# Layer 0 of a two-layer mixture-of-experts block: the outputs of 18 of 43 jobs are added to their tokens' rows in memory by indirect DMAs

## The chip, the cores and the metric

The kernel runs on one core of one Trainium2 chip. The metric is the device time of one execution in microseconds (us), as the median of several runs. The core has TensorE (PE, with its weight loads PEld), VectorE (DVE), ScalarE (ACT), GpSimd (POOL) and SyncE (SP); DMAs are issued here from SP's queue (plain loads) and from POOL's queue (all indirect DMAs and a few plain ones), and run on 16 DMA engines that both queues share.

## The reference, cut to what matters

Two layers follow each other over 256 latent tokens and 256 context tokens of width 1024. Each has a mixer and then a mixture of experts; layer 0 runs its experts over all 512 tokens, and it is the only layer that the change touches. A router picks 8 of 64 experts for each token; every expert is a small gated network, and a token's result is the weighted sum of its 8 experts' outputs, plus that of one shared expert:

```python
def moe_ffn(h, w_router, e_bias, w_gate, w_up, w_down, s_gate, s_up, s_down):
    scores = jax.nn.sigmoid((h @ w_router).astype(jnp.float32))
    _, idx = lax.top_k(scores + e_bias.astype(jnp.float32), TOP_K)
    wts = jnp.take_along_axis(scores, idx, axis=-1)
    wts = wts / wts.sum(-1, keepdims=True) * ROUTE_SCALE
    ...
    def expert_block(args):
        tok, e = args
        xb = h_pad[tok]
        a = jax.nn.silu(xb @ w_gate[e]) * (xb @ w_up[e])
        return a @ w_down[e]
    ...
    routed = jnp.zeros((n_tok + 1, d), h.dtype).at[slot_tok].add(y)[:n_tok]
    shared = (jax.nn.silu(h @ s_gate) * (h @ s_up)) @ s_down
    return routed + shared
```

The line with `.at[slot_tok].add(y)` is what the change does in another way for a part of the outputs.

## The kernel before, in words

**Jobs.** Layer 0 sorts its experts by load and packs them into 43 jobs of 128 slots (class `Plan`). A slot is one token of one expert. A *single* job holds one expert on four lanes of 32 slots; a *pair* job holds two segments, for two experts, of 64 and 64 or of 96 and 32 slots. Single jobs are 0, 1, 2, 6, 11, 15, 20, 25, 29, 34 and 39; all others are pair jobs.

**One iteration of the job loop** (L1685 on) for job j does, in TensorE's order: the gate and up products (`gate_up`, L1291, or `gate_up3` for single jobs, three products of split float32 parts in L161 to L163); four transposes (L1406) of job j+1's gathered rows; a part of the scatter of earlier jobs (L1464); two transposes (L1254) of the activation `a` (ScalarE's `s`, L1238, then VectorE's product, L1239); four more transposes of job j+1 and another part of the scatter; then the down products (L1302, or `down3`). The rows of job j+2 are gathered by an indirect DMA of POOL (`gather`, L1392) from `h2d` in memory, by the token numbers `idx`, into one of two buffers `xg`.

**Combining.** `place` splits a job's output into two float32r parts `yy` (ScalarE casts the high part, VectorE subtracts for the low part, L157) and builds a one-hot matrix `ss` of the slots' tokens (L1441). Every two placed jobs form a group (`GRP` = 2). `scatter` then yields 8 pieces, one for each of 4 token tiles and 2 column halves; a piece is 4 products of 128x128 by 128x512 (two jobs, two parts) and one addition into `acc` by VectorE (L1456). The loop takes 4 pieces in each iteration (`n_piece`), two behind the gate and up products and two behind the transposes of `a`, so that 16 products fall to each job.

**Single jobs** need their weights split: `gu_parts` does it for two rows of blocks at a time (`jj` = 0, 2, 4, 6), with `wh` cast by ScalarE and `wl` subtracted by VectorE (`jj` = 0) or by POOL (`jj` = 2 and 6); `jj` = 4 writes both halves into one tile `parts`. `down3` lets POOL make the `wl` of the second half.

**What sets the order.** TensorE's and SP's instructions stand in the order of the program. The other engines' instructions are ordered by the scheduler. All queues run in order: an instruction that waits holds what stands behind it. SP issues all weight loads and waits for the buffers: 11 `w8` buffers of 1 MB hold weights. Two more pools matter: `t8`, four buffers of 8 KB per partition, for `yy` and `parts`; and `k4`, 13 buffers of 4 KB per partition, for activations, `wh`, `wl`, `acc` and loads of rows.

## Time and profile before

| | |
|---|---|
| median of 3 runs | 1728.12 us (1727.6 to 1729.35) |
| the profiled execution | 1727.71 us, span 1725.8 us |
| busy: PE / PEld | 1620.1 us (94%) / 982.1 us (57%) |
| busy: DVE / ACT / POOL | 802.7 us (47%) / 481.3 us (28%) / 232.7 us (13%) |
| L1464, combining products of both layers | 912 recorded, 243.4 us |
| HBM read / written | 528.44 MB / 6.37 MB |

The page gives each engine's busy time, the span in 40 slices, the DMA queues and the costliest groups of instructions by line. Matmuls are pipelined, so a row's duration overlaps the next row's: what a product costs is read from the distance of the starts. Layer 0's job loop lies roughly between 340 and 970 us of the span, layer 1's from about 1200 us to the end.

### The profile page before, as it was taken

What the parts mean: (1) busy time and instruction counts of PE and PEld (TensorE: products, weight loads), DVE (VectorE), ACT (ScalarE), POOL (GpSimd) and SP (SyncE); (2) the same over time, 40 slices, a digit from 0 to 9 for tenths busy, and PEclk for the clock granted to TensorE, in tenths of its full rate; (3) what the DMA queues carried; (4) which work ended last, traced back from release to release, by engine and by line L of the source; (5) the groups of instructions that cost most, each with busy time, mean ns of one, the idle gap of its engine ahead of it and who ended that gap; (6) DMA issues with size and microseconds to landing.
All of it is one profiled execution on the core that took longest, in us unless ns stands there. A gap on an engine that the chain in (4) does not pass through costs nothing. (4 is left out here: it accounts for less than half of the span.)

```text
span 1725.8 us, 27915 instructions
## 1 busy us (share of the span) xinstructions
PE 1620.1 (94%) x10494; PEld 982.1 (57%) x10494; DVE 802.7 (47%) x2043; ACT 481.3 (28%) x932; POOL 232.7 (13%) x171
## 2 busy tenths in 40 slices
PE   6999999899999999999999799999999999989885
PEld 3765677555455454554545377766656655546553
DVE  2576584655466463443433761446533332222216
ACT  2446211323233232231332242422222111112111
POOL 1014141312022020220211100031100000000001
PEclk9999999999999999999999999999999999999998
DMA  9845755769888999889998567227779999999993
GB/s 330 317 173 184 267 207 207 267 235 349 319 337 304 368 344 345 325 310 361 355 350 335 195 246 260 107 91 315 281 297 421 419 420 420 420 420 420 420 420 141
DMA packets 135400, 530.90 MB, mean 308 GB/s; under 512 B 13488, under 2 KB 22208, under 8 KB 103648
## 3 DMA queue, kind: packets, MB, share of 16 engines
q1 hardware_dynamic: 125776, 500.72, 75.6%
q0 software_dynamic: 9488, 28.37, 4.6%
q8 instruction: 84, 1.38, 0.3%
q14 instruction: 52, 0.43, 0.1%
HBM read 528.44 MB, written 6.37 MB: 310 GB/s over the span
## 5 line engine op out<-in xcount | busy, mean ns | idle before, releaser
L1284 PE MATMUL bank<-w,xT 128*32 128x256 f32 (+2 forms) x2560 | 219.9, 397 | 28.5 <-DMA w<-in_moe_w_up_dram 24.8
L1464 PE MATMUL bank<-yy,ss 128*128 128x512 f32 x912 | 243.4, 404 | 1.9 <-DVE yy L157 1.6
L1302 PE MATMUL bank<-w,aT 128*32 128x512 f32 (+2 forms) x1232 | 233.6, 596 | 1.7 <-ACT aT L1258 1.7
L1291 PE MATMUL bank<-w,xT 128*32 128x512 f32 (+2 forms) x1456 | 233.5, 594 | 0.0
L1239 DVE SCALAR_TENSOR_TENSOR a<-s,wsl,bank 128x256 f32<-128x256 f32 x71 | 34.1, 480 | 398.6 <-ACT s L1238 398.6
L1284 PEld LDWEIGHTS bank<-w,xT 128*32 128x32 f32 (+2 forms) x2560 | 130.3, 125 | 116.2 <-DMA w<-in_moe_w_up_dram 32.4
L1456 DVE TENSOR_TENSOR acc<-acc,bank 128x512 f32<-128x512 f32 x220 | 149.0, 684 | 78.4 <-PE bank L1464 77.5
L1464 PEld LDWEIGHTS bank<-yy,ss 128*128 128x128 f32 x912 | 161.8, 189 | 35.3 <-DVE yy L157 3.4
L1238 ACT ACTIVATE s<-bank 128x256 f32<-128x256 f32 x71 | 27.3, 384 | 508.0 <-PE bank L1291 226.2
L157 DVE TENSOR_TENSOR yy<-bank,yy 128x512 fp32r<-128x512 f32 x140 | 96.2, 688 | 129.3 <-ACT yy L157 129.3
L1291 PEld LDWEIGHTS bank<-w,xT 128*32 128x32 f32 (+2 forms) x1456 | 70.9, 122 | 145.2 <-issue 136.6
L157 ACT CAST yy<-bank 128x512 fp32r<-128x512 f32 x140 | 81.9, 586 | 244.5 <-PE bank L1302 205.3
L1302 PEld LDWEIGHTS bank<-w,aT 128*32 128x32 f32 (+2 forms) x1232 | 67.6, 123 | 118.7 <-issue 110.1
L1392 POOL DMA_INDIRECT xg<-h2d,idx x43 | 49.8, 1158 | 491.6 <-PE bank L1406 388.0
L1214 DVE TENSOR_SCALAR oh<-ib,pos 128x64 bf16<-128x64 bf16 (+3 forms) x428 | 84.2, 272 | 12.9 <-PE bank L1225 12.8
L157 DVE TENSOR_TENSOR wl<-half,wh 128x1024 fp32r<-128x1024 f32 x35 | 49.9, 1429 | 69.2 <-ACT wh L157 69.2
L1384 POOL TENSOR_TENSOR xr<-xr,tmp 128x512 f32<-128x512 f32 x4 | 6.3, 1580 | 537.5 <-DVE tmp L1383 537.5
L157 POOL TENSOR_TENSOR wl<-w,wh 128x1024 fp32r<-128x1024 f32 x28 | 67.9, 2425 | 38.1 <-ACT yy L157 13.9
L161 PE MATMUL bank<-wh,hT 128*128 128x512 f32 x160 | 66.3, 414 | 2.7 <-ACT wh L157 2.1
L163 PE MATMUL bank<-wl,hT 128*128 128x512 f32 x160 | 64.2, 401 | 3.0 <-DVE wl L157 3.0
L162 PE MATMUL bank<-wh,hT 128*128 128x512 f32 x160 | 64.0, 400 | 0.3 <-DVE hT L157 0.2
L1432 PE MATMUL bank<-ohr,h2p 128*128 128x256 f32 x448 | 61.0, 289 | 0.6 <-DVE ohr L1421 0.5
(362 smaller groups left out, 2382.5 us busy)
## 6 DMA issues: line engine op xcount, KB each, us to landing
w<-in_moe_w_down_dram SPq DMA_DIRECT2D x104, 1024.0 KB, 12.9
w<-in_moe_w_gate_dram SPq DMA_DIRECT2D x128, 512.0 KB, 7.0
w<-in_moe_w_up_dram SPq DMA_DIRECT2D x128, 512.0 KB, 7.7
w<-in_moe_w_gate_dram SPq DMA_DIRECT2D x64, 1024.0 KB, 17.4
w<-in_moe_w_up_dram SPq DMA_DIRECT2D x64, 1024.0 KB, 17.3
w<-in_w_mod_dram SPq DMA_DIRECT2D x24, 1024.0 KB, 12.0
half<-in_na_w_in_dram SPq DMA_DIRECT2D x12, 1024.0 KB, 9.4
mh<-in_w_mod_dram SPq DMA_DIRECT2D x12, 1024.0 KB, 5.2
```

The lines of the kernel that those rows point to most:

```text
L157: return A.copy(o_h, src), eng.tensor_sub(o_l, src, o_h.bitcast(F32))
L161: T.matmul(p, xh, wh, start=first, stop=False)
L162: T.matmul(p, xl, wh, start=False, stop=False)
L163: T.matmul(p, xh, wl, start=False, stop=last)
L1214: V.tensor_scalar(oh[:, 32 * lane:32 * (lane + m)], ib[:, off:off + 32 * m], pos[:, t, c:c + 1], None, op0=OP.is_equal)
L1284: T.matmul(p[sl, q * FF:q * FF + FF], xT(j, sl), ws[k][0][q][:, j], start=j == 0, stop=j == NJ - 1, **kw)
L1291: T.matmul(p[sl], xT(j, sl), ws[k][0][j // 4][:, :, j % 4, :], start=j == 0, stop=j == NJ - 1, **kw)
L1302: T.matmul(p[sl], aT[:, j, sl], d[:, n * 512:n * 512 + 512], start=j == 0, stop=j == 1, **kw)
L1392: G.indirect_dma_start(out=x, out_offset=None, in_=h2d[:n2, :], in_offset=bass.IndirectOffsetOnAxis(ap=idx_col, axis=0), bounds_check=n2 - ...
L1432: T.matmul(o, h2p[t][k][:, 2 * q + j], oh[:, t].rearrange("p a b -> p (a b)")[:, :n], start=t == 0 and k == 0, stop=t == nt - 1 and k == 1)
L1456: add = {0: lambda t, r, p: V.tensor_add(acc[t][:, r], acc[t][:, r], p)}
L1464: T.matmul(p, ss[:, t * 128:t * 128 + 128], yy[:, q, r], start=k == 0 and q == 0, stop=k == len(grp) - 1 and q == 1)
```

## The change

Eighteen jobs, the odd ones from 3 to 37 of layer 0 (`sent`), are no longer placed and scattered. `send` copies such a job's output to a tile `yd` (of `t8`) and POOL adds its rows to rows of a tensor `accd` in memory by an indirect DMA with an add, one for each segment: 14 of the 18 are pair jobs with two such DMAs, four are single jobs with one. The second segment's token numbers have to lie on partitions from 0 on, so `second` forms them by small products (`idx2`). Empty slots go to 128 spare rows of `accd`, by `token_index`. `accd` is set to zero by five stores of 512 KB at the start of layer 0. `fetch` reads a tile of 128 tokens back and adds it to `acc`, in each of jobs 38 to 41. With a group of two placed jobs now coming every four jobs, `n_piece` is halved from job 2 to job 39.

```diff
--- before.py
+++ after.py
@@ -1019,6 +1019,7 @@
 
     h2d = dp.tile([512, D], F32, name="h2d")
     xd = dp.tile([512, D], F32, name="xd")
+    accd = dp.tile([640, D], F32, name="accd")
 
     def moe(l, out_of, nt, mp, pre=lambda: None, post=lambda: None):
         n2 = nt * 128
@@ -1186,10 +1187,20 @@
         tok = mp.tile([128, njob], F32, name="tok")
         idx = mp.tile([128, njob], I32, name="idx")
 
+        sent = range(3, njob - 4, 2) if l == 0 else ()
+        idx2 = mp.tile([96, njob], I32, name="idx2")
+
+        def token_index(i_, t_, e_):
+            V.tensor_scalar(e_, t_, 0.0, pid[:t_.shape[0]], op0=OP.is_equal, op1=OP.mult)
+            V.scalar_tensor_tensor(i_, t_, FAR, e_, op0=OP.add, op1=OP.add)
+
         def slot_info(sl, w_, t_, i_):
             V.reduce_sum(w_, sl[:, :, 0:3], axis=AX.X)
             V.tensor_add(t_, sl[:, :, 3], sl[:, :, 4])
-            V.tensor_scalar(i_, t_, FAR, None, op0=OP.add)
+            if l:
+                V.tensor_scalar(i_, t_, FAR, None, op0=OP.add)
+            else:
+                token_index(i_, t_, sl[:, :, 0])
 
         n0 = max(j for j in range(njob) if jobs[j][0][0] < NS) + 1
         group = [0, n0, n0 + 4] + list(range(n0 + 4 + SG, njob, SG)) + [njob]
@@ -1215,12 +1226,25 @@
                                         None, op0=OP.is_equal)
                     ohs[j].append(oh)
 
+            def second(j):
+
+                c, lane, m, off = jobs[j][1]
+                o = p[:32 * m, 256 + 2 * (j - j0):258 + 2 * (j - j0)]
+                for t, oh in enumerate(ohs[j]):
+                    T.matmul(o, oh[:, 32 * lane:32 * (lane + m)], wt[:, t, c, 3:5], start=t == 0, stop=t == nt - 1)
+                tk = mp.tile([96, 2], F32, name="tk2", tag="tk2", bufs=2)[:32 * m]
+                V.tensor_copy(tk, o)
+                V.tensor_add(tk[:, 0:1], tk[:, 0:1], tk[:, 1:2])
+                token_index(idx2[:32 * m, j:j + 1], tk[:, 0:1], tk[:, 1:2])
+
             marks(j0)
             for j in range(j0, j1):
                 if j + 1 < j1:
                     marks(j + 1)
                 yield
                 c0 = min(sg_[0] for sg_ in jobs[j])
+                if j in sent and len(jobs[j]) > 1:
+                    second(j)
                 for t, oh in enumerate(ohs.pop(j)):
                     T.matmul(p[:, (j - j0) * 15:(j - j0) * 15 + 15], oh, wt[:, t, c0:c0 + 3, :],
                              start=t == 0, stop=t == nt - 1)
@@ -1352,6 +1376,8 @@
             xgs = [k4([128, D], f"xg{i}") for i in range(2)]
             for x in xgs:
                 V.memset(x, 0.0)
+            for t in range(nt + 1):
+                G.dma_start(accd[t * 128:t * 128 + 128, :], xgs[t % 2])
 
         def both(xs, j0, xT):
             for k in range(2):
@@ -1452,6 +1478,22 @@
                     V.tensor_mul(y, ps[n], times[:, r])
                 split(yy[:, 0, r], yy[:, 1, r], y)
             return yy, ss if ss is not None else tokens(t_col)
+
+        def send(j, ps):
+
+            y = t8([128, D], "yd", F32)
+            A.copy(y[:, :512], ps[0])
+            V.tensor_copy(y[:, 512:], ps[1])
+            for k, (c, lane, m, off) in enumerate(jobs[j]):
+                i_ = (idx2 if k else idx)[:32 * m, j:j + 1]
+                G.indirect_dma_start(out=accd[:, :], out_offset=bass.IndirectOffsetOnAxis(ap=i_, axis=0),
+                                     in_=y[32 * lane:32 * (lane + m)], in_offset=None, compute_op=OP.add)
+
+        def fetch(t):
+
+            y = k4([128, D], "ad")
+            S.dma_start(y, accd[t * 128:t * 128 + 128, :])
+            V.tensor_add(acc[t], acc[t], y)
 
         add = {0: lambda t, r, p: V.tensor_add(acc[t][:, r], acc[t][:, r], p)}
 
@@ -1583,7 +1625,6 @@
         for sg_ in jobs:
             passes.append(3 if l == 0 and len(sg_) == 1 and sg_ is not jobs[0] else 4)
         grp, sc = [], iter(())
-        n_piece = -(-2 * nt // GRP)
         over = overflow()
         LA = 3 if l == 0 else 2
         with tc.manual_schedule(engines={mybir.EngineType.SP, mybir.EngineType.PE}):
@@ -1684,6 +1725,9 @@
                     early[c] = expert_dn(c, ds(S.value_load(ordi[0:1, c:c + 1], min_val=0, max_val=NE - 1), 1))
             for j in range(njob - l):
                 segs = jobs[j]
+                n_piece = -(-2 * nt // GRP)
+                if sent and 2 <= j < njob - 3:
+                    n_piece //= 2
                 experts([sg_[0] for sg_ in segs])
                 if j == njob - 1:
                     g2s = [modrow(l, "g2", s) for s in range(nt // 2)]
@@ -1751,7 +1795,12 @@
                     for _ in sc:
                         pass
                     add_x = add[0] = fold(g2s)
-                grp.append(place(ps, tok[:, j:j + 1]))
+                if j in sent:
+                    send(j, ps)
+                else:
+                    grp.append(place(ps, tok[:, j:j + 1]))
+                if sent and 0 <= j - (njob - 5) < nt:
+                    fetch(j - (njob - 5))
                 if len(grp) == GRP or j >= njob - 2:
                     for _ in sc:
                         pass
```

The scheduler and the pools place the new instructions. In the rows below, a wait on DMASW is for the landing of a DMA that POOL issued, one on DMAHW for one that SP issued, and the digit tells the semaphore; `_49` is a suffix of all.

POOL's queue around job 20, a single job, before (`xg` the gathers, `wl` the low parts of job 20's weights):

```order
L1392 DMA xg_1813<-h2d,idx 128x1024 [waits DMASW5_49,PE_49]
L1392 DMA xg_1812<-h2d,idx 128x1024 [waits DMASW6_49,PE_49]
L157 TENSOR_TENSOR wl<-w_5744,wh 128x1024 [waits DMAHW3_49,DMAHW2_49,Activation_49]
L157 TENSOR_TENSOR wl<-w_5747,wh 128x1024 [waits DVE_49,DMAHW4_49,PE_49,DMAHW5_49,Activation_49,Pool_49]
L1392 DMA xg_1813<-h2d,idx 128x1024 [waits DMASW7_49,PE_49]
L157 TENSOR_TENSOR wl<-w_5750,wh 128x1024 [waits DMAHW6_49,DVE_49,Activation_49]
```

The same place with the change; the two rows on `accd` are the sends of job 19, which use the semaphores DMASW4 and DMASW5:

```order
L1418 DMA xg_1814<-h2d,idx 128x1024 [waits DMASW7_49,PE_49]
L157 TENSOR_TENSOR wl<-w_5659,wh 128x1024 [waits DMAHW3_49,DMAHW2_49,Activation_49]
L1489 DMA accd<-yd,idx 640x1024 [waits DMASW1_49,DVE_49,Activation_49]
L157 TENSOR_TENSOR wl<-w_5662,wh 128x1024 [waits DMAHW4_49,DMAHW5_49,PE_49,Pool_49]
L1489 DMA accd<-yd,idx_1813 640x1024 [waits DMASW4_49]
L1418 DMA xg_1815<-h2d,idx 128x1024 [waits DMASW2_49,PE_49]
L157 TENSOR_TENSOR wl<-w_5665,wh 128x1024 [waits DMAHW6_49,Activation_49]
```

The second send waits for the first one's landing (DMASW4), and a gather and job 20's last `wl` stand behind it.

ScalarE's order at the same place, the end of job 19 and job 20's split weights (`wh`, `parts`), before:

```order
L157 CAST wh<-w_5747 128x1024 [waits DMAHW5_49,DMAHW4_49,Activation_49]
L157 CAST yy<-bank 128x512 [waits PE_49]
L157 CAST parts<-w_5747 128x1024
L157 CAST yy<-bank 128x512 [waits PE_49]
L1238 ACTIVATE s<-bank 128x256 [waits PE_49]
```

With the change:

```order
L157 CAST wh<-w_5662 128x1024 [waits DMAHW5_49,DMAHW4_49,Activation_49]
L1485 COPY yd<-bank 128x512 [waits DMASW1_49,DMASW0_49,PE_49]
L157 CAST parts<-w_5662 128x1024 [waits DMASW4_49,DMASW5_49,DVE_49,Activation_49]
L1262 ACTIVATE s<-bank 128x256 [waits PE_49]
L1437 COPY xT<-bank 128x512 [waits PE_49]
```

`parts` waited for nothing that POOL issues and now waits for DMASW4 and DMASW5, both sends of job 19; the `s` of job 20 stands behind it.

SP's queue between job 38's down weights and job 39's gate and up weights, before (`ordi` is the list of experts):

```order
L1043 DMA w_8012<-in_moe_w_down_dram 128x2048 [waits DMAHW2_49,PE_49]
L1059 TENSOR_LOAD ordi
L1059 ISA x2
L1038 ISA
L1038 DMA w_8109<-in_moe_w_gate_dram 128x1024 [waits DMAHW3_49,PE_49]
```

With the change:

```order
L1044 DMA w_7692<-in_moe_w_down_dram 128x2048 [waits DMAHW2_49,PE_49]
L1495 DMA ad<-accd 128x1024 [waits DMAHW3_49,DMASW7_49,DMASW6_49]
L1060 TENSOR_LOAD ordi
L1060 ISA x2
L1039 ISA
L1039 DMA w_7780<-in_moe_w_gate_dram 128x1024 [waits DMAHW4_49,PE_49]
```

The first `fetch` (`ad`) stands ahead of job 39's loads; DMASW6 and DMASW7 are the two sends of job 37.

## Rows read from the trace of the kernel before

**Rows 1.** Window 400 to 960 us (length, busy us of each engine, PEclk, DMA share, GB/s)

```profile
400.00:960.00 560.00, 559.27 (x3284) 297.67 (x3282) 271.44 (x570) 153.69 (x263) 96.32 (x60) 1.00 0.91 340
```

**Rows 2.** Timeline of PE, jobs 36 and 37 (start us, us, engine, line, operation)

```profile
858.99 7.07 PE L1291 MATMUL bank<-w,xT 128*32 128x512 f32 x64
...
866.00 0.66 PE L1406 MATMUL bank<-head,xg 128*128 128x128 f32 x4
...
866.41 2.10 PE L1464 MATMUL bank<-yy,ss 128*128 128x512 f32 x8
...
868.35 0.39 PE L1254 MATMUL bank<-head,a 128*128 128x128 f32 x2
...
874.52 0.65 PE L1291 MATMUL bank<-w,xT 128*64 128x512 f32 x2
```

**Rows 3.** Line 1464 from 340 to 970 us (duration ns min/median/max)

```profile
L1464 PE MATMUL bank<-yy,ss x672: 387/393/762, 344.9 to 957.3; 128*128 128x512 f32 x168
```

**Rows 4.** Timeline of DVE in job 36

```profile
866.64 0.48 DVE L1239 SCALAR_TENSOR_TENSOR a<-s,wsl,bank 128x256 f32<-128x256 f32 x1 [6.19 <-ACT s L1238]
```

**Rows 5.** Timeline of PE, slot products between jobs

```profile
509.62 0.36 PE L1225 MATMUL bank<-wt,oh 128*128 128x15 bf16 x8
509.91 7.09 PE L1291 MATMUL bank<-w,xT 128*64 128x512 f32 x32
```

**Rows 6.** Tile xg from 660 to 760 us, six gathers among loads

```profile
DMA to landing us min/median/max: 4.7/8.2/9.3
```

**Rows 7.** Tile xg from 260 to 300 us, two gathers on quiet engines

```profile
DMA to landing us min/median/max: 4.3/4.8/5.2
```

**Rows 8.** Tile xd, whole span: four stores issued by POOL

```profile
DMA to landing us min/median/max: 3.0/7.1/8.2
```

**Rows 9.** DMA queues and issues, 400 to 960 us (packets, MB, share; KB, landing)

```profile
q0 software_dynamic: 5328, 14.92, 7.1%
...
w<-in_moe_w_up_dram SPq DMA_DIRECT2D x106, 512.0 KB, 7.8
w<-in_moe_w_down_dram SPq DMA_DIRECT2D x53, 1024.0 KB, 9.4
```

**Rows 10.** Timeline of ACT and DVE in single job 34

```profile
828.71 1.05 ACT L157 CAST parts<-w 128x1024 fp32r<-128x1024 f32 x1
829.97 0.59 ACT L157 CAST yy<-bank 128x512 fp32r<-128x512 f32 x1 [0.21 <-PE bank L1302]
...
830.17 1.21 DVE L157 TENSOR_TENSOR parts<-w,parts 128x1024 fp32r<-128x1024 f32 x1
```

**Rows 11.** Timeline of SP's queue, job 38's last loads

```profile
874.63 3.90 SPq L1043 DMA_DIRECT2D w<-in_moe_w_down_dram  x2
```

**Rows 12.** Timeline of PE, end of job 37

```profile
889.97 0.60 PE L1291 MATMUL bank<-w,xT 128*64 128x512 f32 x2
```

**Rows 13.** Timeline of PE and POOL in job 34

```profile
829.83 0.50 PE L161 MATMUL bank<-wh,xT 128*128 128x512 f32 x1
...
831.48 2.39 POOL L157 TENSOR_TENSOR wl<-w,wh 128x1024 fp32r<-128x1024 f32 x1 [2.52 <-ACT yy L157]
...
839.86 2.42 POOL L157 TENSOR_TENSOR wl<-w,wh 128x1024 fp32r<-128x1024 f32 x1
```

**Rows 14.** Timeline of POOL before layer 0's first normalization

```profile
190.52 2.88 POOL L152 DMA_DIRECT2D row<-rowsd  x5
```

**Rows 15.** DMA issues from 188 to 194 us

```profile
row<-rowsd POOLq DMA_DIRECT2D x5, 512.0 KB, 11.2
```

**Rows 16.** Timeline of DVE and PE in layer 0's normalizations

```profile
205.92 1.37 DVE L993 TENSOR_TENSOR tmp<-bank,row 128x512 f32<-128x512 f32 x2 [9.34 <-PE bank L163]
...
232.23 3.16 PE L1097 MATMUL bank<-rw,h2T 128*128 128x64 f32 x16 [2.98 <-ACT h2T L1017]
```

**Rows 17.** Windows of 4 us around a stop of PE

```profile
232.00:236.00 4.00, 3.77 (x18) 3.68 (x19) 4.00 (x4) 2.17 (x4) 3.98 (x3) 0.60 0.70 200
236.00:240.00 4.00, 4.00 (x11) 3.08 (x11) 4.00 (x19) 0.00 (x0) 1.93 (x2) 0.54 0.67 243
```


## The prediction

> **What bounds the kernel now.** I read first the busy page, then one window over most of layer 0's job loop, then single jobs in the timeline, then the queues of SP and POOL. In the window the reader is to see that TensorE is the bound: 559.27 of 560 us busy at full clock, while the 16 DMA engines are at 0.91 [rows 1]. So time goes if TensorE's work shrinks, as long as nothing else makes TensorE wait.
>
> A pair job takes 15.53 us (858.99 to 874.52): gate and up 7.0, four transposes, 8 combining products (L1464), two transposes of `a`, four more, again 8 products, and the down products [rows 2]. The 8 products take 866.41 to 868.35, 1.94 us, 0.2425 us each. Below, T is the moment when a sent job's down product ends.
>
> **Removed.** 18 jobs lose their 16 products: 288 of them, 288 x 0.2425 = **-69.8 us**. Of the 43 jobs' 688, 672 lie between 340 and 970 us [rows 3], where nearly every one is on the path. No gap opens in their place: each iteration keeps 4 products behind gate and up and 4 behind `a`, and a pair job's `a` is ready 1.12 us after gate and up (867.12 against 866.00) [rows 2, 4], while the transposes ahead and 4 products of 0.2425 take 0.4 + 1.0. VectorE's fewer additions and splits hide behind TensorE.
>
> **Added products.** `second` brings 14 x 4 = 56 tiny products. The nearest row, 8 of L1225's, holds TensorE for 0.29 us (509.62 to 509.91) [rows 5]: 0.036 each, **+2 us**. Its 56 VectorE steps have cover, VectorE being busy 271 of 560 us [rows 1].
>
> **What a send costs until it lands** is the unknown that decides. No add in memory is in this trace. The nearest row is the gather, also an indirect DMA of POOL in 4 KB rows: median 8.2 us from issue to landing among the weight loads, 4.8 when the engines are quiet [rows 6, 7]. Below, a plain POOL store of 512 KB lands in 3.0 at best [rows 8]; above, two loaded gathers, 16.4, if reading the old sum and adding it cost a second pass. I take **7.5 loaded and 5 quiet**: a half send has half the gather's rows (about 1.1 us less, since a 1 MB load lands 2.3 us after a 512 KB one [rows 9]), and reading the old rows gives part of that back.
>
> **Added waits.** Two sends of a job write the same tensor, so POOL holds the second until the first has landed: both are down at T+0.8+7.5+0.1+7.5 = T+15.9 among loads (0.8 for the copy to `yd`, as a `yy` cast starts 0.21 after the product and takes 0.59 [rows 10]). Who is behind them:
>
> - Job 20's `parts`. The four t8 buffers now hold two `yy` in scatter, one waiting, and the sent `yd`; the order rows show `parts` waiting for both sends of job 19. TensorE wants `parts` 12 products in, at T+2.9. It stops, the loads drain, so the second send lands at the quiet price: T+13.4; cast 1.05, subtraction 1.21 [rows 10], 0.5 of slack: T+15.2. **+12.3.**
> - The first `fetch` stands in SP's queue ahead of job 39's loads, and SP gets there early: job 38's last load was issued at 874.63 to 878.53 while job 37 ended at 889.97 [rows 11, 12]. SP then stands until job 37's sends land, at quiet prices T+10.9. Loads, split and start of job 39: about T+19.3 instead of T+13.6. The second `fetch` waits for a k4 buffer with job 40's loads behind it, some 4 more. **+10.**
> - POOL's last `wl` of a single job stands behind both sends. Before, it ran 839.86 to 842.28, 12.4 us into job 34, which began at 829.83 [rows 13], hence wanted at T+10.5. Job 6: first send after the second `wl` (T+4.1), landing T+11.6, second issue 1.0, gather 1.0, `wl` 2.4: T+16.1, 5.6 late. Job 34, where the send is ahead of that `wl`: 2.3 late. **+8.**
> - `parts` of 11 and 15, and the `yy` cast ahead of `parts` in 24 and 28, wait for sends of the job before (9, 13, 23, 27). From T+15.9 they end 1.2 late (twice) and 1.8 late (twice) against T+16.5. **+6.** In the other even jobs (4, 8, 32, 36) the late `yy` cast is covered by the next gate and up, until T+20.6.
> - Gathers stand ahead of the sends that follow them in POOL's queue and have a job of slack: 0.
> - The five zeroing stores precede the row loads of the first normalization: 2.88 us of issue as for the five row loads [rows 14], and 2.6 MB ahead of them on a queue whose five loads landed after 11.2 us median [rows 15]. Five us later, VectorE's start at 205.92 slips, and TensorE already waits for ScalarE's copy behind it at 232.23 [rows 16]. Between 0 and 8: **+4.**
> - Clock. After TensorE's stop of 2.98 us before 232.23 [rows 16] the granted clock was 0.60 and 0.54 over 8 us [rows 17], the low level, costing (0.40 + 0.46) x 4 = 3.4 us. The three stops over 3 us (jobs 20, 39, 6): **+10.**
> - Weights. They are issued some 24 us before use or more (874.63 for a product after 889.97 + 8.6) [rows 11, 12]; between stops TensorE gains up to 14 x 1.94 = 27 us on them: **+4.**
>
> Sum: -69.8 + 2 + 12.3 + 10 + 8 + 6 + 4 + 10 + 4 = **-13.5 us**. The profiled execution took 1727.7 us, within 0.5 of the median 1728.1, so I predict **1714 us**. With sends of 6 and 4.5 us the waits shrink to about 44 in all (1702); with 8 and 5.1 they grow to about 62 (1720). That is the forecast's own range.
>
> **Rivals.**
>
> 1. *Slower: t8's buffers decide.* Place: the wait of `yy` and `parts` for both sends. Each us of landing is paid twice in every such wait. From about 8.4 us loaded on, the four waits of jobs 11, 15, 25 and 29 each pass 3 us and bring the low clock too, and the gain is gone. At 10 (6 quiet): job 20 15.8, job 39 11.7, `wl` 12.9, the four 26, the four other `yy` 6, start, `second` and weights 10, clock eight times 27: 109 - 70 = +40, 1767 us. For it: the gather is at 8.2 without any adding, and its slowest there took 9.3 [rows 6]. Against: half the rows.
>
> 2. *The DMA engines become the bound.* They are busy 0.91 x 560 = 510 us where TensorE would want about 500. The 16 sends there carry 8.4 MB; at the software queue's 7.1% of 560 us for 14.92 MB [rows 9], 2.67 us per MB, that is 22 us with one reading, 45 with two. Then the stretch takes 532 to 555 us, and with 6 for start and `second` the kernel 1706 to 1729. For it: 0.91 already. Against: part of that share is time in which few packets are outstanding. The Trainium skill, "Collectives: The Full Stack", section "The bandwidth ceiling: the fold count and why AG ≠ RS ≠ AR", says that an addition in the DMA path is slow because it reads two sources, not because it adds. By that rule the upper end holds, 1729 us, no change; no row here shows an adding DMA.
>
> 3. *Faster: the sends are quick.* If a send lands like the quiet store (3 to 4 us), only jobs 20 (7) and 39 (6), 2 of `wl`, 4 of start and `second` and 8 of clock remain: 27 - 70 = -43, 1685 us. The loaded gather speaks against it. The Trainium skill, "DMA: Bandwidth & Descriptors", section "Anatomy of one DMA — SWDGE (gpsimd) path", fits 2.0 us plus bytes over 436 GB/s; an estimate by it is 2.6 us for 256 KB and would give this rival's time. The gather's rows disagree with it among loads: 8.2 us where it would say about 3.
>
> **How the numbers follow.** Two measurements of this kernel can be told apart from about 0.2%, 3.5 us. Forecast (1702 to 1720) 0.43, slower by late sends 0.33, DMA bound near 1729 0.12, quick sends 0.12. Faster by over 0.2%: 0.43 + 0.12 = 0.55; within: 0.12; slower: 0.33. The range reaches half into the quick case and over the slower case up to 10 us per send: 1694 to 1767, leaving out about 0.06 and 0.12.
>
> **What would show it.** Right: 288 fewer L1464 products; the send's median landing among loads at 6 to 8 us; TensorE stopped about 12 us in job 20 on ScalarE's `parts`, and again before job 39 on weights; SP's longest wait at the fetch; dips of the clock at those places. Wrong: landing above 8.4 us, with stops in jobs 11, 15, 25 and 29 of over 3 us; or DMA share near 1.0 with TensorE waiting for weights in ordinary jobs; or no stop at 20, which would mean that `parts` got another buffer.

## The result and the profile after

The changed kernel takes 1789.86 us in the median of 4 runs (1789.09 to 1794.05), the kernel before 1727.86 beside it: a ratio of 1.0365, 95% interval 1.0348 to 1.0381. The forecast was 1714 us, in a range of 1694 to 1767. The profiled execution of the change took 1789.63 us, with a span of 1787.8 us and a mean granted clock of 0.956 (before 1725.8 us and 0.982).

The same window as in [rows 1], now of the change:

```profile
400.00:960.00 560.00, 492.01 (x2852) 242.22 (x2852) 196.00 (x503) 137.67 (x236) 142.04 (x88) 0.94 0.88 320
```

TensorE is busy 492 us there, not 559, and its clock is 0.94. The DMA engines are at 0.88, less than before: they are not the bound. What TensorE waited for between 340 and 1000 us (line, what it waited for, us in all, times, longest):

```profile
PE bank L1249 <- DVE tk L1236: 29.0, 12, 6.6
PE bank L163 <- POOL wl L157: 20.6, 12, 8.2
PE bank L161 <- ACT parts L157: 16.9, 3, 13.3
PE bank L161 <- ACT wh L157: 8.1, 1, 8.1
PE bank L1315 <- DMA w<-in_moe_w_up_dram: 4.5, 3, 2.3
PE bank L163 <- DVE parts L157: 4.3, 3, 3.5
```

The last of these, 4.3 us, is old (the kernel before has 3.9 of it). The other five, 79 us, are new, and only the 4.5 us on L1315 are a wait for weights.

The saving is there too. Line 1464 is L1506 now, and the page counts 624 of its products against 912, 288 fewer. Jobs 36 and 37 again, as in [rows 2]:

```profile
900.64 7.07 PE L1315 MATMUL bank<-w,xT 128*32 128x512 f32 x64
...
914.32 7.09 PE L1315 MATMUL bank<-w,xT 128*64 128x512 f32 x32
```

They are 13.68 us apart, not 15.53. The sends' landing, from issue on (tile `accd`, 340 to 1000 us):

```profile
DMA to landing us min/median/max: 3.6/7.6/12.9
```

The table gives, for the jobs that matter, the distance in us from a job's transposes of `a` to those of the next job, each read from the starts in PE's timeline (L1254 before, L1278 after). Job 36 is an undisturbed one. The last columns belong to experiments below.

| from job | before | change | e1 | e2 | e3 | e6 | e13 |
|---|---|---|---|---|---|---|---|
| 4 | 17.19 | 24.85 | 17.51 | 24.82 | 25.50 | 17.52 | 17.31 |
| 6 | 15.49 | 26.71 | 20.88 | 26.64 | 16.13 | 17.91 | 14.45 |
| 8 | 16.64 | 21.44 | 17.94 | 21.18 | 19.85 | 18.00 | 15.12 |
| 10 | 14.23 | 19.12 | 21.30 | 19.04 | 20.42 | 15.81 | 15.78 |
| 14 | 14.16 | 20.15 | 19.56 | 21.42 | 16.87 | 17.22 | 15.13 |
| 19 | 14.24 | 28.81 | 13.75 | 27.61 | 29.01 | 12.43 | 13.41 |
| 24 | 14.05 | 16.63 | 16.60 | 18.36 | 16.93 | 16.28 | 14.74 |
| 28 | 14.05 | 16.48 | 16.34 | 18.31 | 17.10 | 16.37 | 14.76 |
| 36 | 15.54 | 13.70 | 13.69 | 13.69 | 13.69 | 13.69 | 13.70 |
| 38 | 14.05 | 23.63 | 22.27 | 16.69 | 23.30 | 14.72 | 14.75 |
| 39 | 15.05 | 24.39 | 25.48 | 17.70 | 24.44 | 16.48 | 16.53 |
| 0 to 42, all | 657.86 | 706.53 | 684.04 | 699.49 | 675.50 | 626.98 | 609.40 |

So of the 62 us between the two profiled spans, 6.4 arise before job 0 (its transposes are at 308.78 before, 315.20 after), 48.7 in the loop, and the last 7 behind it. In the loop an undisturbed distance is 1.84 shorter, which for 36 jobs is 66 us; the new waits, with the low clock behind them, therefore cost 48.7 + 66 = 115 us. Where they are, in the timelines of the change:

**Jobs 4, 8, 10 and 14: a slot product waits for VectorE.** Slot products (L1249, and L1234 in `second`) work out the tokens and weights of later jobs' slots from one-hot marks `oh`, which VectorE makes; they stand between jobs up to 684 us of the span. POOL's sends of job 3, then ScalarE, VectorE and TensorE at the end of job 4:

```profile
379.65 1.52 POOL L1489 DMA_INDIRECT accd<-yd,idx  x1 [4.90 <-issue]
389.08 1.35 POOL L1489 DMA_INDIRECT accd<-yd,idx  x1 [7.91 <-DMA accd<-yd,idx]
```

```profile
396.37 1.07 ACT L157 CAST yy<-bank 128x512 fp32r<-128x512 f32 x2 [8.29 <-DMA accd<-yd,idx]
```

```profile
396.98 0.69 DVE L157 TENSOR_TENSOR yy<-bank,yy 128x512 fp32r<-128x512 f32 x1 [7.88 <-ACT yy L157]
397.59 1.25 DVE L1225 TENSOR_SCALAR oh<-ib,pos 128x64 bf16<-128x64 bf16 x8
398.75 0.15 DVE L1236 COPY tk<-bank 64x2 f32<-64x2 f32 x1
```

```profile
392.07 0.29 PE L1234 MATMUL bank<-wt,oh 128*64 128x2 bf16 x4
398.95 0.36 PE L1249 MATMUL bank<-wt,oh 128*128 128x15 bf16 x8 [6.59 <-DVE tk L1236]
```

The first send went out at 379.65 and landed 9.2 us later, the second followed at 389.08, and ScalarE's cast `yy` waited for it until 396.37, 18.5 us after job 3's down products ended at 377.9. VectorE's subtraction for `yy` stood behind the cast, and behind that the marks `oh` and the copy `tk` of a later job's slots. TensorE's next slot product (L1249) waited for `tk`, 6.59 us. It stands at the end of job 4, ahead of job 5's gate and up products. In job 8 the order is the same. At the end of jobs 10 and 14 it is the next job's `parts` that waits for a landing on ScalarE and holds VectorE; the rows are those of job 10:

```profile
510.28 1.04 ACT L157 CAST parts<-w 128x1024 fp32r<-128x1024 f32 x1 [3.89 <-DMA accd<-yd,idx]
```

```profile
512.70 0.36 PE L1249 MATMUL bank<-wt,oh 128*128 128x15 bf16 x8 [5.13 <-DVE tk L1236]
```

Job 32 shows the other side. Its `yy` waited as long, but no slot product stands behind it any more, and TensorE ran from its down products straight into job 33's gate and up products:

```profile
861.84 1.07 ACT L157 CAST yy<-bank 128x512 fp32r<-128x512 f32 x2 [8.85 <-DMA accd<-yd,idx]
```

```profile
856.79 7.09 PE L1315 MATMUL bank<-w,xT 128*64 128x512 f32 x32
```

**Job 20** (ScalarE; the wait is for both sends of job 19) and **job 6** (POOL's last `wl` behind both sends of job 5, then TensorE):

```profile
669.57 1.04 ACT L157 CAST parts<-w 128x1024 fp32r<-128x1024 f32 x1 [16.41 <-DMA accd<-yd,idx]
```

```profile
423.00 1.46 POOL L1489 DMA_INDIRECT accd<-yd,idx  x1 [1.74 <-issue]
431.42 1.42 POOL L1489 DMA_INDIRECT accd<-yd,idx  x1 [6.95 <-DMA accd<-yd,idx]
...
434.21 2.35 POOL L157 TENSOR_TENSOR wl<-w,wh 128x1024 fp32r<-128x1024 f32 x1
```

```profile
436.61 0.79 PE L163 MATMUL bank<-wl,aTh 128*128 128x512 f32 x1 [8.17 <-POOL wl L157]
```

**Jobs 38 and 39:** SP's queue, with the first and second read of the sums, and TensorE:

```profile
918.00 0.33 SPq L1044 DMA_DIRECT2D w<-in_moe_w_down_dram  x1
939.46 0.34 SPq L1495 DMA_DIRECT2D ad<-accd  x1
...
943.16 0.51 SPq L1044 DMA_DIRECT2D w<-in_moe_w_down_dram  x1
958.80 0.33 SPq L1495 DMA_DIRECT2D ad<-accd  x1
```

```profile
949.72 0.80 PE L161 MATMUL bank<-wh,xT 128*128 128x512 f32 x1 [8.07 <-ACT wh L157]
...
978.48 3.59 PE L1315 MATMUL bank<-w,xT 128*32 128x512 f32 x26 [2.28 <-DMA w<-in_moe_w_up_dram]
```

SP's own waits ahead of the reads, from 340 to 1000 us:

```profile
SPq L1495 <- DMA accd<-yd,idx: 21.1, 1, 21.1
SPq L1495 <- PE bank L163: 15.0, 1, 15.0
```

SP stood still from 918 to 939, until job 37's sends had landed, and again from 943.7 to 958.8 ahead of the second read, until products of job 39 (L163) were done; TensorE stopped 8.07 us for job 39's weights and then for job 40's.

**The start:** POOL, and the router products of [rows 16], whose wait is now 8.78 us:

```profile
193.75 2.12 POOL L1380 DMA_DIRECT2D accd<-xg  x4 [0.77 <-DVE xg L1378]
195.86 1.57 POOL L152 DMA_DIRECT2D row<-rowsd  x3
202.87 0.53 POOL L152 DMA_DIRECT2D row<-rowsd  x1 [5.43 <-DMA accd<-xg]
```

```profile
237.97 3.68 PE L1098 MATMUL bank<-rw,h2T 128*128 128x64 f32 x16 [8.78 <-ACT h2T L1017]
```

**The clock.** Windows of 4 us behind the stop of job 6 (columns as in [rows 1]):

```profile
436.00:440.00 4.00, 2.50 (x12) 1.78 (x13) 1.93 (x10) 1.17 (x2) 0.56 (x1) 0.50 0.81 254
440.00:444.00 4.00, 3.87 (x24) 1.23 (x27) 2.52 (x19) 0.00 (x0) 0.00 (x0) 0.50 0.26 107
444.00:448.00 4.00, 4.00 (x42) 1.16 (x37) 0.00 (x0) 0.00 (x0) 0.00 (x0) 0.97 0.23 47
```

The granted clock was 0.50, the low level, for some 7.5 us after TensorE came back, which costs about 3.7 us. Behind the stop of 13.3 us in job 20 it was 0.50 and 0.71 in two windows. Behind the stops of jobs 4, 8 and 14 and the one before job 39 it was back at 0.72 to 0.84 in the second window, and behind that of job 10 at 1.00. Counted from the end of each stop, these seven cost about 19 us of low clock together, an estimate from such windows.

### The profile page after: what moved, and what is told of

Same layout as the page of the kernel before. It is cut to its first block, busy times and chain, and to the rows that moved or that the text cites. A ratio compares the mean times of both kernels' runs of the same rounds, so it can differ in the third digit from the quotient of the medians.

```text
span 1787.8 us, 27435 instructions
## 1 busy us (share of the span) xinstructions
PE 1590.0 (89%) x10262; PEld 947.5 (53%) x10262; DVE 740.7 (41%) x2002; ACT 469.6 (26%) x914; POOL 286.2 (16%) x208
## 5 line engine op out<-in xcount | busy, mean ns | idle before, releaser
L1315 PE MATMUL bank<-w,xT 128*32 128x512 f32 (+2 forms) x1456 | 242.8, 612 | 4.5 <-DMA w<-in_moe_w_up_dram 4.5
L1308 PEld LDWEIGHTS bank<-w,xT 128*32 128x32 f32 (+2 forms) x2560 | 131.0, 124 | 116.9 <-DMA w<-in_moe_w_up_dram 34.4
L1506 PE MATMUL bank<-yy,ss 128*128 128x512 f32 x624 | 179.2, 413 | 1.3 <-DVE yy L157 1.0
L1315 PEld LDWEIGHTS bank<-w,xT 128*32 128x32 f32 (+2 forms) x1456 | 74.0, 125 | 156.6 <-issue 155.1
L1498 DVE TENSOR_TENSOR acc<-acc,bank 128x512 f32<-128x512 f32 x148 | 101.1, 685 | 68.2 <-PE bank L1506 67.8
L157 DVE TENSOR_TENSOR yy<-bank,yy 128x512 fp32r<-128x512 f32 x104 | 71.2, 688 | 132.6 <-ACT yy L157 132.5
L1506 PEld LDWEIGHTS bank<-yy,ss 128*128 128x128 f32 x624 | 108.4, 191 | 22.6 <-DVE yy L157 2.7
L157 ACT CAST yy<-bank 128x512 fp32r<-128x512 f32 x104 | 60.5, 586 | 201.7 <-PE bank L1326 128.5
L1225 DVE TENSOR_SCALAR oh<-ib,pos 128x64 bf16<-128x64 bf16 (+3 forms) x428 | 79.2, 259 | 8.3 <-PE bank L1249 8.0
L1489 POOL DMA_INDIRECT accd<-yd,idx x32 | 47.6, 1488 | 153.7 <-DMA accd<-yd,idx 85.9
L163 PE MATMUL bank<-wl,hT 128*128 128x512 f32 x160 | 64.1, 401 | 3.0 <-DVE wl L157 3.0
## 6 DMA issues: line engine op xcount, KB each, us to landing
w<-in_moe_w_down_dram SPq DMA_DIRECT2D x104, 1024.0 KB, 13.6
half<-in_na_w_in_dram SPq DMA_DIRECT2D x12, 1024.0 KB, 10.9
```

Of the source, the lines that this page charges most:

```text
L157: return A.copy(o_h, src), eng.tensor_sub(o_l, src, o_h.bitcast(F32))
L163: T.matmul(p, xh, wl, start=False, stop=last)
L1225: V.tensor_scalar(oh[:, 32 * lane:32 * (lane + m)], ib[:, off:off + 32 * m], pos[:, t, c:c + 1], None, op0=OP.is_equal)
L1308: T.matmul(p[sl, q * FF:q * FF + FF], xT(j, sl), ws[k][0][q][:, j], start=j == 0, stop=j == NJ - 1, **kw)
L1315: T.matmul(p[sl], xT(j, sl), ws[k][0][j // 4][:, :, j % 4, :], start=j == 0, stop=j == NJ - 1, **kw)
L1489: G.indirect_dma_start(out=accd[:, :], out_offset=bass.IndirectOffsetOnAxis(ap=i_, axis=0), in_=y[32 * lane:32 * (lane + m)], in_offset=No ...
```

## The experiments

Each kernel ran beside the kernel before on one chip; a ratio is to that, with its 95% interval, and what a run gains or loses is taken from the difference of two such ratios. Four repairs were tried alone first, each aimed at one wait.

**e1: a buffer of its own for `yd`.**

```diff
+        ybuf = w8([128, 2, D], "yd") if l == 0 else None
+
         def send(j, ps):
-            y = t8([128, D], "yd", F32)
+            y = ybuf[:, j // 2 % 2]
```

> The copy `yd` of a sent job goes to a buffer of its own (one weight buffer held for layer 0, its two halves in turn), no longer to one of the four t8 buffers; weights keep 10 buffers instead of 11 there. Buffer theory: all waits of ScalarE's `yy` and `parts` for the landing of sends go, and with them TensorE's stops on the slot products (6.6, 3.7, 5.1 and 5.4 us), on `parts` in job 20 (13.3 us) and in jobs 25 and 29, and the low clock behind them: about 50 us less, 1740 us. Rival, the sends' traffic or their adding is what costs: the stops turn into waits for weights at the same places and the time stays above 1775 us.

Measured: 1764.51 us, 1.0205 (1.0188 to 1.0222), 27 us less than the change, about half of what was expected. The stops on the slot products and in job 20 went: the distance from job 4 fell from 24.85 to 17.51, from job 8 from 21.44 to 17.94, from job 19 from 28.81 to 13.75. In jobs 25 and 29 the wait for `parts` went too, but one of 1.66 us for `wh` came in its place, and the distances from jobs 24 and 28 stayed (16.60 and 16.34). The waits for weights did not grow (4.8 us, 4.5 before). Part of the gain came back at single jobs, at waits for `wl` and for VectorE's `parts`: the distances from jobs 10, 15 and 20 rose by 2.2, 2.9 and 3.2 us. What POOL does to VectorE shows in e1's rows at the start of job 11, VectorE and then POOL:

```profile
493.86 2.43 DVE L1225 TENSOR_SCALAR oh<-ib,pos 128x128 bf16<-128x128 bf16 x1
496.21 2.38 DVE L1195 SCALAR_TENSOR_TENSOR idx<-tk 64x1 int32<-64x1 f32 x1
498.52 1.59 DVE L1225 TENSOR_SCALAR oh<-ib,pos 128x128 bf16<-128x128 bf16 x10
```

```profile
493.86 4.71 POOL L157 TENSOR_TENSOR wl<-w,wh 128x1024 fp32r<-128x1024 f32 x2 [3.24 <-DVE wl L157]
```

One mark `oh` and one index of 64 elements took 2.4 us each while POOL subtracted its two `wl`; once POOL had ended at 498.57, ten marks took 1.59 us together, 0.16 each. The subtraction for `parts` came that much later, and TensorE waited 4.09 us for it. The Trainium skill, "SBUF — State Buffer", section "SBUF: two separate sides", says that GpSimd shares one pair of ports with VectorE's instructions in a two-port mode, or with two inputs from SBUF while the GpSimd instruction reads SBUF, and that the one that starts first holds the pair for its whole instruction while the other is blocked; these rows agree as far as they go: each of the two took as long as one `wl` (4.71 / 2 = 2.36). In which mode `oh` ran, no row tells.

**e2: the reads later.**

```diff
-                if sent and 0 <= j - (njob - 5) < nt:
-                    fetch(j - (njob - 5))
+                if sent and j in (njob - 3, njob - 2):
+                    for t in range(2):
+                        fetch(2 * (j - (njob - 3)) + t)
```

> The four reads of the sums are issued two ahead of job 41's loads and two ahead of job 42's, not one ahead of each of jobs 39 to 42. Theory that SP's queue is held at the first read until job 37's sends have landed: TensorE's stop of 8.1 us before job 39 and the weight waits of job 40 go, 15 to 22 us less, about 1771 us. Rival, the reads wait for k4 buffers that come free late, and hold SP wherever they stand: less than 5 us gained, the stop now before job 41 or 42.

Measured: 1783.69 us, 1.0313 (1.0287 to 1.0338), 9 us less. Jobs 38 and 39 are 13.6 us shorter together, the weight waits are gone, and no stop appeared before job 41 or 42. The total fell short of the 15 to 22 us expected: jobs 14, 24 and 28, which wait for sends, were 1.3 to 1.8 longer in this execution.

**e3: `wl` on VectorE.**

```diff
-            split(wh, wl, w[0][jj // 4][:, :, jj % 4:jj % 4 + 2], G if jj in (2, 6) else V)
+            split(wh, wl, w[0][jj // 4][:, :, jj % 4:jj % 4 + 2], V)
...
-                wh, wl = w_parts([128, D], w[1][:, j, :], G if j else V)
+                wh, wl = w_parts([128, D], w[1][:, j, :], V)
```

> All low parts `wl` of single jobs' weights are subtracted by VectorE, none by POOL. Theory that POOL's in-order queue delays them behind the sends: the stops on POOL's `wl` go (8.2 us in job 6, 2.8 and 0.9 in job 34, 1.1 in each other single job) with some 4 us of low clock behind job 6's: 15 to 24 us less, about 1770 us. Rival, VectorE's queue is held by the same waits for sends: under 5 us gained, the stops now on VectorE's `wl`.

Measured: 1757.32 us, 1.0170 (1.0153 to 1.0188), 34 us less, more than the 15 to 24 us of the stops on `wl`. Job 6 fell from 26.71 to 16.13. Job 1, where the change stopped 3.5 us for VectorE's `parts` and not for `wl`, fell from 19.92 to 14.30, in line with e1's rows: POOL's blocking of VectorE is part of the rest. How large a part, this run does not show. The stops of jobs 4, 10 and 19 stayed.

**e4: sends without adding.** 

```diff
-                                     in_=y[32 * lane:32 * (lane + m)], in_offset=None, compute_op=OP.add)
+                                     in_=y[32 * lane:32 * (lane + m)], in_offset=None)
```

> The sends write their rows without adding (the sums of the 18 jobs are left out: a token keeps the last row written). If adding in memory is cheap: landing 7 to 7.7 us in the median as before, and the time within 8 us of the change's 1790 us. If the addition costs a second pass over the rows: landing about 4 us, the waits of `yy` and `parts` shorter by twice the difference, and the time 25 us or more lower.

Measured: 1773.01 us, 1.0258 (1.0241 to 1.0275), 18 us less, and between the two expectations. The landing, as above:

```profile
DMA to landing us min/median/max: 3.2/6.4/12.6
```

Adding costs some 1.2 us of a landing of 7.6, not a second pass; the runs that add, with one send of a job at a time, have medians of 7.6 to 8.0. Two landings stand in a row in a wait, so some 2.4 us should come off each: job 19's distance fell by 2.0 to 26.83, job 4's by 2.8 to 22.06. The Trainium skill, "Collectives: The Full Stack", section "The bandwidth ceiling: the fold count and why AG ≠ RS ≠ AR", says of a ReduceScatter in a ring of ranks that it runs at half an AllGather's rate because its addition reads two sources. The prediction carried that over to the sends; their landing, 1.2 times as long and not twice, does not show it.

**e5: the zeroing on SP.**

```diff
-            for t in range(nt + 1):
-                G.dma_start(accd[t * 128:t * 128 + 128, :], xgs[t % 2])
...
                 hps[t] = norm_h2(l, t, ps, rw_, mp)
+                if l == 0 and t == 2:
+                    for k in range(nt + 1):
+                        S.dma_start(accd[k * 128:k * 128 + 128, :], xgs[k % 2])
```

> The five stores that zero the sums leave POOL's queue and stand in SP's queue behind the third normalization's store of rows, so the row loads of the first normalization no longer stand behind them. Theory that they delay those loads: TensorE's stop of 8.8 us at 238 us shrinks to the 3.0 of the kernel before, layer 0's jobs start 6 us earlier, 1784 us. Rival, the stores cost the same wherever they stand: the job loop starts as late, or job 0 waits for its gather instead, 1790 us.

Measured: 1786.36 us, 1.0332 (1.0315 to 1.0349), 6 us less, an interval that just meets the change's. In the profiled execution job 0 began 8.3 us earlier (306.92 against 315.20), which bears out the theory of the start. That execution was the longest of the four (1789.7 us), and its loop took the gain back: it was 715.87 us long, not 706.53, in jobs 24, 28, 34 and 39 above all. In 24 and 28 the stops on `parts`, which waits for sends, were 2.9 and 2.4 us, not 2.2 and 1.4.

**e6 and e7: all four; and with the reads in `ybuf`.** e6 is e1, e2, e3 and e5 together; e7 also has

```diff
-            y = k4([128, D], "ad")
+            y = ybuf[:, t % 2]
```

> Own buffer for `yd`, all `wl` on VectorE, the reads two ahead of each of jobs 41 and 42, the zeroing on SP: the four repairs together. Theory that the products saved (67 us in the loop) are real and all of the loss is these waits: taking for every job the best of the single repairs, the loop is 25 us shorter than in the kernel before, with some 4 us left at the start and in layer 1: about 1706 us. Rival, the DMA engines: as TensorE gains on the weights, waits for weights appear in ordinary pair jobs and hold the time at 1725 us or above.

> As the four repairs together, but the reads of the sums go to the two halves of the buffer of `yd` and not to k4 buffers. If waits for k4 buffers still hold SP at the reads: 3 to 8 us below the four repairs together, in jobs 40 to 42. If not: the same within 3 us, or later by the second pair of reads, which waits for the addition of the first.

Measured: e6 1703.38 us, 0.9860 (0.9843 to 0.9878); e7 1702.95, 0.9856 (0.9840 to 0.9873). The sum job by job held (1706 expected), the DMA rival did not, and the reads' buffer made no difference. In e6 the landing was not shorter than in the change (median 8.0 us): what went is the waiting for it. TensorE's two main waits in e6, 340 to 940 us:

```profile
PE bank L1249 <- DVE tk L1236: 11.3, 11, 1.7
PE bank L161 <- ACT wh L157: 6.0, 4, 1.7
```

11.3 us on `tk` are left although no send is late any more.

**e8: control.** e3's edit made in the kernel before.

> Control: the kernel before with all `wl` of single jobs on VectorE, none of the change. If moving `wl` helps only because of the sends in POOL's queue: within 3 us of 1728 us. If POOL's subtractions beside VectorE's cost time by themselves: 5 to 12 us less.

Measured: 1724.81 us, 0.9981 (0.9971 to 0.9990), 3.3 us less, just over the first expectation and under the second. So of e3's 34 us about a tenth has nothing to do with the sends; job 1 alone is 3.8 us shorter here.

**e9: a second tensor for the second segments.**

```diff
+    accd2 = dp.tile([640, D], F32, name="accd2")
...
-                G.indirect_dma_start(out=accd[:, :], ...
+                G.indirect_dma_start(out=(accd2 if k else accd)[:, :], ...
```

(`accd2` is zeroed as `accd` is in e5.)

> The change, but the second send of a pair job goes to a second tensor, zeroed by SP (it is not read back: the second segments' sums are left out). The waits of `yy`, `parts` and the buffers are unchanged; only the second send no longer waits for the first one's landing. Theory that the two landings in a row are what makes the buffers late: the stops shrink by one landing, 6 to 7 us each where they are longer (job 20 from 13 to about 7, job 6's 8 and job 4's 6.6 to under 2), with the low clock behind them 30 to 40 us less, about 1755 us. Rival, two sends under way at once take twice as long each, because the queue or the engines move them no faster: under 10 us less.

Measured: 1747.88 us, 1.0113 (1.0096 to 1.0130), 44 us less, where 30 to 40 were expected. POOL's two sends of job 3, and the landing:

```profile
378.24 1.52 POOL L1490 DMA_INDIRECT accd<-yd,idx  x1 [4.89 <-issue]
380.06 1.35 POOL L1490 DMA_INDIRECT accd<-yd,idx  x1 [0.30 <-DVE oh L1226]
```

```profile
DMA to landing us min/median/max: 3.5/8.1/12.7
```

The second send goes 1.8 us after the first instead of 9.4, and a landing takes 8.1 us instead of 7.6: two under way at once hardly slow each other. Job 4's stop on `tk` is under 1.2 us, and job 6's on `wl` 1.5. TensorE's stop in job 20 is 9.4 us, not the 7 expected.

**e10 and e11: all but one repair.** e6 without the own buffer; e6 with `wl` on POOL.

> The repairs together without the own buffer of `yd` (reads late, zeroing on SP, `wl` on VectorE). Buffer theory: the stops of jobs 4, 8, 10, 14 and 20 are back, some 32 us over the 1703 us of all four: about 1735 us. Rival, with the other repairs made, the waits are covered: under 8 us over it.

> The repairs together with `wl` left on POOL. From the run with the own buffer alone, taken job by job: the single jobs lose 1.2 us each on the last `wl`, jobs 6, 10, 15, 20 and 34 3 to 6 us, job 1 six: some 35 us over the 1703 us of all four, about 1738 us. Rival, POOL was late only because of sends whose waits are now gone elsewhere: under 10 us over it.

Measured: e10 1733.89 us, 1.0044 (1.0031 to 1.0058); e11 1745.27, 1.0098 (1.0081 to 1.0114): 32 and 41 us over e6, where 32 and 35 were expected. So these two repairs are each needed with the others made; the kernel was not run without the other two. TensorE's two main waits in e10:

```profile
PE bank L161 <- ACT parts L157: 20.2, 5, 14.5
PE bank L1249 <- DVE tk L1236: 17.6, 11, 6.5
```

That e10's total fits is in part luck, because its places do not: jobs 4 and 19 are back (24.96 and 29.33) and make up 24 of the loop's 30 us, but jobs 8, 10 and 14 stand at 17.28, 16.67 and 16.47, together no longer than in e6. In e3, whose edits differ from e10's only in the zeroing and in the reads at the end, they took 19.85, 20.42 and 16.87. So what a late send costs in these jobs differs between two kernels that are alike there; that the moment of its landing decides is likely and was not shown.

**e12 and e13: the copies `tk` behind a group's last products**, in the change, and in e7.

```diff
+            seconds = []
+
             def second(j):
...
-                tk = mp.tile([96, 2], F32, name="tk2", tag="tk2", bufs=2)[:32 * m]
+                seconds.append((j, o, m))
+
+            def second_index(j, o, m):
+                tk = mp.tile([96, 2], F32, name="tk2", tag="tk2", bufs=2)[:32 * m]
...
+            for s_ in seconds:
+                second_index(*s_)
             sm = mp.tile([128, SG, 5, 3], F32, name="sm", tag="sm", bufs=1)
```

> The change, but the second segments' indices are copied out of the bank (`tk`) once, after the last products of a group of slots, and no longer between the products of two jobs. Theory that a group's next slot products (L1249) wait for the copy `tk` in VectorE's queue because both stand in one bank: the 12 stops on `tk`, 29.0 us in all, go where VectorE had only `tk` outstanding, and stay in part in jobs 4 and 8, where the marks `oh` stand behind the same `yy` too: 15 to 25 us less, about 1770 us. Rival, the products wait for the marks `oh` in any case: the stops stay with another name, under 6 us less.

> The four repairs, the reads in the buffer of `yd`, and the copies `tk` after the last products of a group. With no late sends left, the 11 stops on `tk` of 1.0 to 1.7 us, 11.3 us in all, should go: 1703 less 8 to 12, about 1693 us. Rival, VectorE's marks `oh` come as late as `tk` did: under 3 us less.

Measured: e12 1777.64 us, 1.0298 (1.0281 to 1.0316), 12 us less, short of the 15 expected. No stop on `tk` is left; the distance from job 8 fell to 15.13 and from job 10 to 14.51, and job 4's stop stayed with the marks `oh` (6.1 us), as the theory said. Jobs 24 and 28 came out 2.8 and 4.9 longer, at ScalarE's `wh`, and job 19 2.1; why stays open. e13: 1686.21 us, 0.9766 (0.9742 to 0.9791), 16 us below e7, where 8 to 12 were expected, and 40 us below the kernel before. Its main waits from 340 to 940 us, and the window:

```profile
PE bank L161 <- ACT wh L157: 7.6, 5, 1.7
PE bank L410 <- DVE xr L1844: 5.4, 1, 5.4
PE bank L162 <- DVE aTl L157: 4.1, 9, 0.5
PE bank L163 <- DVE wl L157: 4.0, 5, 1.5
```

```profile
400.00:960.00 560.00, 529.92 (x3188) 263.79 (x3186) 262.80 (x590) 157.46 (x269) 96.08 (x70) 0.98 0.99 375
```

(L410 is behind the loop.) No wait on `tk`, on POOL or on a send is left among them, and none for weights, though the DMA engines are at 0.99. They may be the next bound, but no run tests it: between 1300 and 1700 us, in layer 1, the kernel before moved 414 GB/s at a share of 1.00, against 375 here.

## Why the prediction was wrong

- **The step that failed** is the sentence that in the other even jobs "the late `yy` cast is covered by the next gate and up, until T+20.6" (T is the end of the sent job's down products). In job 4 the cast came at T+18.5, inside that limit, and TensorE had stopped at T+14.4 already, so even the T+15.9 of the sum would have been too late. The cover counts only who needs `yy`. VectorE, in order, needed it first, and behind its subtraction stood `oh` and `tk` for slot products that TensorE runs ahead of that gate and up. The prediction named what is queued behind waiting instructions on POOL and SP, and not on VectorE. Jobs 32 and 36, where no slot products stand, took 13.69 and 13.70 us: there the cover held. The same queue turned the "1.2 late" of jobs 11 and 15 into stops of 5.1 and 5.4 us.
- **What it cost.** The distances from jobs 4, 8, 10 and 14 are 31 us over those before less the 1.84 saved (24.85 - 17.19 + 1.84 and so on), those from 24 and 28 another 9, where 6 stood in the sum. Not all of the 31 is the late sends: in e6, where no send is late, 14 of them are left, in part the waits on `tk` of the next point. e1 shows the cause for jobs 4, 8 and 19; for jobs 10 and 14 the rows of the change show the queue, and the single cost is not settled, as e10 and e3 differ there.
- **`second` was mis-sized**, by the same oversight. Its 4 products take 0.29 us a job, but VectorE's copy `tk` reads the bank that the next slot products write, and TensorE waited for it 1.0 to 1.7 us at a time in e6, 11.3 us in all, with no send late. "Its 56 VectorE steps have cover" was wrong; 2 stood in the sum, and e13, which moves the copies, gives 16 us back.
- **`wl` was mis-sized:** 8 taken. Job 6 stopped 8.2 us, not 5.6. The single jobs stopped 1.1 us each on the last `wl`, with sends late or not (e11 has these stops too), which was not in the sum; nor were POOL's subtractions beside VectorE's. With e3 all of it is 34 us.
- **The reads were mis-sized:** the first was as predicted (issued at T+11.5 against T+10.9), but the second held SP 15 us, not 4. Jobs 38 and 39 cost 22 us, where 10 stood; e2 gives 14 of them back.
- **The clock was mis-sized:** three stops over 3 us assumed, seven new ones found. The price of one was about right (at most 3.7 us, where 3.4 was taken); together they cost about 19 us, where 10 stood.
- **The start:** +4 taken, 6.4 measured, and e5 shows that the zeroing ahead of the row loads was the cause.
- **The saving was right.** There are 288 products fewer, at 1.84 us for 8 of them against the 1.94 assumed, so 66 us in the loop against 69.8.
- **The landing was right in the median**, 7.6 us against 7.5 taken; job 3's two sends, behind which job 4 stopped, took 9.2 and 7.2. The 1.1 us taken off a gather for its half size goes by two loads 2.3 us apart, and [rows 9] show two that are 1.6 apart, which would give 0.8.
- **Job 20 was right:** +12.3 taken, a stop of 13.3 us measured, with both landings in a row. Two errors partly cancel in it: the second send took 5.9 us and not 5, and the stop ended with ScalarE's cast, without the subtraction of 1.21 that the sum has. e9 lets the two landings overlap and leaves 9.4.
- **Rival 1 had the sign, by another mechanism.** Its threshold, a landing of 8.4 us, was not passed in the median. Of its four waits over 3 us, jobs 11 and 15 did stop that long, through VectorE's queue; jobs 25 and 29 stopped 2.2 and 1.4 us.
- **The DMA rival** is refuted for this kernel: the share is 0.88 in the change, while e6 and e13 run faster at 0.96 and 0.99 over the same window, and e6's 1703 us lies below the 1706 that the rival allowed.

Of the signs named for "right", the products, the landing, the stop in job 20, the stop before job 39 and the dips of the clock all came. They check the terms that are in the sum and say nothing of a wait that it takes as covered. No single step carries the 76 us between the forecast and the result. The largest are the waits at slot products behind jobs 4, 8, 10 and 14 (31 us, of which about 17 are late sends), `wl` (34 us with e3, 8 taken) and `second` (16 us, 2 taken); they overlap and can't be added up.

Not settled: the last 7 us behind the loop. Some 2.2 of them lie between the first and the second transposes of `a` in layer 1, where the granted clock was 0.93 and not 1.00; in e13 it was 1.00 there, and the stretch took as long as in the kernel before. Another 3 lie behind the last VectorE instruction, where the span goes on for 8.4 us instead of 5.4. The causes stay open.

## What to carry to other kernels

When a wait is added to an instruction, list what stands behind it on its own engine and on every engine that takes its result, and look for the next thing the bounding engine needs from any of them, not only for the user of the late value. A transfer that nobody waits for was cheap here only with a buffer of its own for its source; taken from a pool that the main chain also draws on, its latency can go straight onto the path (here 27 us for one 8 KB buffer per partition in e1, 32 in e10). The idea itself was sound: with its waits removed it is 2.3% faster than the kernel before, 0.2% of which e8 gives without it.

## What the runs showed of the hardware

- The change's 32 indirect DMAs that add rows of 4 KB into memory, 288 KB each on average, landed in 7.6 us in the median among weight loads, and in 6.4 without the add (e4). With two under way at once the median was 8.1 (e9).
- Two VectorE instructions of the kind that took 0.16 us behind them took 2.4 us each while POOL subtracted 128x1024 (e1).
- TensorE's list of waits for 400 to 960 us names no load of weights in e6 and e13, at DMA shares of 0.96 and 0.99.
